# A hybrid decoder layer: output projection by pairs of column blocks, adaLN sums kept in their weight tiles, the second norm of tile 0 among tile 1's last products

## The chip, the cores and the metric

The kernel runs on one core of one Trainium2 chip. The metric is device time in microseconds, from runs of the whole program; the profile is of one further execution. The engines are called TensorE (PE, matrix products), VectorE (DVE), ScalarE (ACT), GpSimd (POOL) and SyncE (SP, which here issues most DMAs).

## What is computed

One layer for 256 tokens of width 2048, all in float32, followed by a final RMSNorm:

```
mod = silu(c) @ w_ada + b_ada          -> shift, scale, gate for the mixer and for the FFN
h   = rms_norm(x) * (1 + scale_m) + shift_m
p   = h @ w_in                         -> column blocks for a GLA group (4 heads) and an HGRN2 group (8 heads)
y   = concat(GLA heads, HGRN2 heads) @ w_out
x   = x + gate_m * y
h   = rms_norm(x) * (1 + scale_f) + shift_f
x   = x + gate_f * (silu(a) * u) @ w_ffn_out,   a, u = split(h @ w_ffn_in)
out = rms_norm(x)
```

Each head's output is normed and multiplied by silu of its gate block before the concatenation.

## The kernel before

**Products.** The 256 tokens are two tiles of 128 (t = 0, 1). A float32 operand is written as a high part, rounded to the fast matrix format, and a low part, the remainder; a product is the sum of three matmuls (`products_of`, L243 to L256: low times high, high times high, high times low). Weights come from memory in half-chunks of 128 x 1024 (`load_ahead`, L216, issued on SyncE's queue, at most 5 ahead), ACT makes the high part (L209) and DVE or POOL the low part (L210). `low_on_pool` (L233) says by the number of the half-chunk which of the two engines takes it: 0 to 111 are the input projection, 112 to 143 the output projection, from 144 on the feed-forward weights. `next_half` (L193) keeps the splits 3 half-chunks ahead of the products, and further ahead for the few named in `EARLY_SPLIT`, whose parts lie in slabs instead of the 4 split buffers.

**Order.** A scheduler orders the instructions of each engine by the order in the program and by its own estimate of when operands and buffers are there; each engine then runs its list in order. `issue_after` places an instruction behind another on the same engine. Buffers of a pool are shared by tag: 33 slabs of 4 KB per partition, 5 raw weight tiles, 4 raw tiles of the adaLN weights, 2 PSUM tiles of two banks (`mm_bank`, `mm_apart`, L258 to L267), 3 single PSUM banks (`bank`) and 1 for the adaLN sums.

**Input projection.** Six groups of rows (`K_GROUPS`), in each of them all column blocks; the gate blocks g0, g1, s0, s1 come last (L722 to L734). Beside the last group and these blocks run three tasks (`gla_group`, `hg_group(0)`, `hg_group(1)`), each advanced once per unit of products. They compute the heads' scores on DVE, ACT and PE, the heads' outputs (`head_outputs`), and in `gated` (L547) the product with the gate block (L549), four transposes per pair of 128 columns on PE (L283) and the split into y (L271, L272). The slabs of y are taken in `gated`.

**adaLN stream.** `ada_sums` (L109) streams 512 columns of w_ada in 8 loads of two row blocks and accumulates row block times c on DVE into one PSUM bank (L127); the last accumulation goes into a slab. `ada_channel` (L134) reduces it over the partitions with matmuls against ones (L147) and makes shift and scale; `ada_gate` (L161) starts from a slab that POOL sets to zero and the bias is loaded into, and reduces with a matmul (L180). `Spread` deals out the steps of this stream evenly over the units of products: 51 steps over 30 units for the second norm's first four column blocks and the mixer's gate.

**Output projection.** All tasks are run to their end in the program (L735) before it. Then four column blocks of 512, one after the other, each over the row groups 8, 12, 0, 4 (`OUT_ORDER`: the HGRN2 halves g0, g1, then the GLA halves s0, s1). After a block, DVE multiplies by the gate and adds x (L754, L755), ACT squares and sums (L757). After block 3, whose last two row groups are one unit and whose tile 1 is done in two halves of 256 columns, come the sums, the power -1/2 on POOL (L295) and the diagonal matrices (L353) for both tiles. The first two row blocks of h for the feed-forward part are then made by matmuls against the diagonal (`normed`, L359), the affine step on ACT and DVE (L420, L418) and the split:

```python
    for t in range(NT):
        c = slice(t * P, (t + 1) * P)
        for j in range(2):
            normed(pts[j][:, :, c], x1[0][:, t], 2 * j, diag_y[t])
            for i in range(2):
                affine(pts[j][:, i, c], 1, 2 * j + i, j == 1)
        for j in range(2):
            h2_made = split_pair(pts[j][:, :, c], h2[j][..., c])
```

**Feed-forward part.** The first six pairs of hidden blocks are computed in four row groups (q = 0 to 3), with the adaLN stream beside them; the first unit takes both blocks of a pair at once (L794 to L797). The rest and the second projection follow, then the final norm.

Of the kernel before, what the change touches and what calls it, by code (L numbers as in the profile page):

```python
# [17 lines left out]
F32 = mybir.dt.float32  # L18
# [4 lines left out]
ALU = mybir.AluOpType  # L23
# [27 lines left out]
MIXER_LOW = (76, 116)  # L51

# [6 lines left out]
def hybrid_layer(ctx: ExitStack, tc: tile.TileContext, x, c, w_ada, b_ada, norm_mix_w, w_in,  # L59
# [49 lines left out]
    def ada_sums(name, out, bias, *parts):  # L109
# [5 lines left out]
        for k0 in range(0, KT, 2):  # L115
# [13 lines left out]
            yield  # L129
# [4 lines left out]
    def ada_channel(which, ka, kb, then=None):  # L134

        n = kb - ka
        sums = slab(f"sums{which}_{ka}", (P, 2, n * P))
        shift, scale = (lambda v, s=s: v[..., 3 * which + s, ka * P:kb * P] for s in range(2))
        if n == 2:
            yield from ada_sums(f"ada{which}_{ka}", sums.rearrange("p s n -> p (s n)"), None, shift, scale)  # L140
        else:
            for s, part in enumerate((shift, scale)):
                yield from ada_sums(f"ada{which}_{ka}_{s}", sums[:, s], None, part)
        pa = pad.tile([P, 2, n], F32, tag="acc", name=f"pada{which}_{ka}")
        for s in range(2):
            for j in range(n):
                nc.tensor.matmul(pa[:, s, j:j + 1], sums[:, s, j * P:(j + 1) * P], ones[:, 0:1],  # L147
                                 start=True, stop=True)
# [11 lines left out]

    def ada_gate(which, half, store):  # L161
# [3 lines left out]
        nc.sync.dma_start(out=gate[0:1], in_=b_ada_v[:, 3 * which + 2, 1024 * half:1024 * (half + 1)]  # L165
                          .rearrange("o (b n) -> o b n", b=2))
        for b in range(2):
            c0 = 1024 * half + 512 * b
            yield from ada_sums(f"adag{which}_{half}_{b}", gate[:, b], gate[:, b],
                                lambda v: v[..., 3 * which + 2, c0:c0 + 512])  # L170
        passes = [(ones, gate)]
        if which:
            hi, lo = (split.tile([P, 2, 512], F32R, tag=n, name=f"{n}_gate{half}") for n in ("hi", "lo"))
            nc.scalar.activation(hi, gate, AF.Copy)
            nc.vector.tensor_tensor(out=lo, in0=gate, in1=hi.bitcast(F32), op=ALU.subtract)
            passes = [(ones_r, lo), (ones_r, hi)]
        for b in range(2):
            pg = pad.tile([P, 512], F32, tag="acc", name=f"pgate{which}_{half}_{b}")
            for i, (one, part) in enumerate(passes):
                nc.tensor.matmul(pg, one, part[:, b], start=i == 0, stop=i == len(passes) - 1)  # L180
# [10 lines left out]
    last_mm = [None]  # L191

    def next_half():  # L193

        i = n_used[0]
        n_used[0] += 1
        while True:
# [537 lines left out]
    while tasks:  # L735
        advance()
# [174 lines left out]
```

## Time and profile before

| | |
|---|---|
| median of 3 runs | 1284.21 us (1283.5 to 1285.42) |
| the profiled execution | 1284.97 us |
| its span, first to last instruction | 1283.1 us |
| TensorE matmuls, busy | 1228.3 us |
| VectorE, busy | 882.7 us |
| ScalarE, busy | 601.5 us |
| GpSimd, busy | 355.1 us |
| mean granted TensorE clock | 0.990 |

The profile is of one execution, and its times are from the start of the span. A wait is put down to the instruction whose signal came last. The granted clock is the share of full speed that TensorE was allowed in a stretch. The busy time of TensorE is modelled from starts and sizes, so starts are the surer thing to read.

### The profile page before, as it was taken

What the parts mean: (1) busy time and instruction counts of PE and PEld (TensorE: products, weight loads), DVE (VectorE), ACT (ScalarE), POOL (GpSimd) and SP (SyncE); (2) the same over time, 40 slices, a digit from 0 to 9 for tenths busy, and PEclk for the clock granted to TensorE, in tenths of its full rate; (3) what the DMA queues carried; (4) which work ended last, traced back from release to release, by engine and by line L of the source; (5) the groups of instructions that cost most, each with busy time, mean ns of one, the idle gap of its engine ahead of it and who ended that gap; (6) DMA issues with size and microseconds to landing.
All of it is one profiled execution on the core that took longest, in us unless ns stands there. A gap on an engine that the chain in (4) does not pass through costs nothing.

```text
span 1283.1 us, 16035 instructions
## 1 busy us (share of the span) xinstructions
PE 1228.3 (96%) x5811; PEld 1025.5 (80%) x5811; DVE 882.7 (69%) x1055; ACT 601.5 (47%) x746; POOL 355.1 (28%) x168
## 2 busy tenths in 40 slices
PE   2999999999997999899999999899999999999996
PEld 2888888888886788688888888788888888888886
DVE  5499986579999873658793799796555454445554
ACT  5644444496643444455343455434334444444443
POOL 4677766500000477365656000000000000000010
PEclk9999999999998999899999999999999999999998
DMA  9999999745577797599897687795666556655662
GB/s 342 350 341 353 355 333 317 253 132 164 178 260 236 262 391 269 190 356 339 309 366 242 214 280 268 253 357 192 197 192 193 185 190 194 187 188 186 196 196 84
DMA packets 178535, 323.65 MB, mean 252 GB/s; under 512 B 12688, under 2 KB 29684, under 8 KB 178456
## 3 DMA queue, kind: packets, MB, share of 16 engines
q1 hardware_dynamic: 175800, 317.33, 73.1%
q10 hardware_dynamic: 2464, 5.24, 1.2%
q8 instruction: 46, 0.75, 0.2%
q14 instruction: 33, 0.27, 0.1%
q0 software_dynamic: 192, 0.06, 0.0%
HBM read 320.49 MB, written 2.10 MB: 251 GB/s over the span
## 4 chain that ended last, share of the span: by engine, by line
PE 60%; DMA 2%; DVE 2%; issue 1%; POOL 1%; ACT 1%; SPq 0%; POOLq 0%; ACTq 0%; DVEq 0%
PE mm_f L256 18%; PE mm_f L254 18%; PE mm_f L255 18%; PE mm_out L254 1%; PE mm_out L255 1%; PE mm_out L256 1%; DMA wada<-in_w_ada_dram 1%; PE pthid L283 1%; DMA raw_f_b<-in_w_ffn_in_dram 1%; PE pth L359 1%; DVE lo_f_a L210 1%; DVE accada L127 0%; POOL lo_out_b L210 0%; PE pada L147 0%; DMA fw<-in_final_norm_w_dram 0%
## 5 line engine op out<-in xcount | busy, mean ns | idle before, releaser
L209 ACT ACTIVATE hi_f_a<-raw_f_a 128x1024 fp32r<-128x1024 f32 x132 | 140.1, 1061 | 337.8 <-PE mm_f L255 319.3
L210 DVE TENSOR_TENSOR lo_f_a<-raw_f_a,hi_f_a 128x1024 fp32r<-128x1024 f32 x116 | 151.8, 1309 | 208.7 <-ACT hi_f_a L209 208.1
L127 DVE SCALAR_TENSOR_TENSOR accada<-wada,c_act,accada 128x512 f32<-128x512 f32 x224 | 168.6, 753 | 18.0 <-DMA wada<-in_w_ada_dram 12.9
L209 ACT ACTIVATE hi_f_b<-raw_f_b 128x1024 fp32r<-128x1024 f32 x132 | 140.0, 1061 | 52.5 <-PE mm_f L255 44.3
L254 PE MATMUL mm_f<-hi_f_a,h 128*128 128x512 f32 x352 | 138.9, 395 | 1.1 <-DVE pf L805 0.6
L256 PE MATMUL mm_f<-lo_f_a,h 128*128 128x512 f32 x352 | 138.2, 393 | 0.0
L255 PE MATMUL mm_f<-hi_f_a,h 128*128 128x512 f32 x352 | 137.8, 391 | 0.0
L256 PE MATMUL mm_f<-lo_f_b,h 128*128 128x512 f32 x352 | 137.6, 391 | 0.0
L254 PE MATMUL mm_f<-hi_f_b,h 128*128 128x512 f32 x352 | 137.1, 390 | 0.0
L255 PE MATMUL mm_f<-hi_f_b,h 128*128 128x512 f32 x352 | 137.1, 389 | 0.0
L854 POOL TENSOR_TENSOR xr<-xr,fw 128x512 f32<-128x512 f32 x6 | 8.8, 1462 | 458.0 <-ACT junkf L851 458.0
L210 DVE TENSOR_TENSOR lo_f_b<-raw_f_b,hi_f_b 128x1024 fp32r<-128x1024 f32 x99 | 122.4, 1237 | 16.9 <-ACT hi_f_b L209 9.6
L210 POOL TENSOR_TENSOR lo_f_b<-raw_f_b,hi_f_b 128x1024 fp32r<-128x1024 f32 x33 | 80.1, 2427 | 44.9 <-ACT hi_f_b L209 44.9
L127 DVE SCALAR_TENSOR_TENSOR accadag<-wadag,c_act,accadag 128x512 f32<-128x512 f32 x112 | 84.2, 751 | 3.4 <-DMA wadag<-in_w_ada_dram 1.8
L254 PEld LDWEIGHTS mm_f<-hi_f_a,h 128*128 128x128 f32 x352 | 66.7, 189 | 15.7 <-ACT hi_f_a L209 1.4
L256 PEld LDWEIGHTS mm_f<-lo_f_a,h 128*128 128x128 f32 x352 | 66.5, 189 | 13.8
L255 PEld LDWEIGHTS mm_f<-hi_f_a,h 128*128 128x128 f32 x352 | 66.5, 189 | 13.6
L255 PEld LDWEIGHTS mm_f<-hi_f_b,h 128*128 128x128 f32 x352 | 66.1, 188 | 13.8
L256 PEld LDWEIGHTS mm_f<-lo_f_b,h 128*128 128x128 f32 x352 | 66.1, 188 | 13.5
L254 PEld LDWEIGHTS mm_f<-hi_f_b,h 128*128 128x128 f32 x352 | 66.1, 188 | 13.3
L254 PE MATMUL mm_f<-hi_f_b,hid 128*128 128x512 f32 (+1 forms) x186 | 70.6, 380 | 3.7 <-ACT hi_f_b L209 3.7
L256 PE MATMUL mm_f<-lo_f_b,hid 128*128 128x512 f32 (+1 forms) x186 | 70.8, 381 | 0.2 <-DVE lo_f_b L210 0.2
(392 smaller groups left out, 2755.3 us busy)
## 6 DMA issues: line engine op xcount, KB each, us to landing
wada<-in_w_ada_dram SPq DMA_DIRECT2D x96, 512.0 KB, 6.0
raw_f_a<-in_w_ffn_in_dram SPq DMA_DIRECT2D x88, 512.0 KB, 4.5
raw_f_b<-in_w_ffn_in_dram SPq DMA_DIRECT2D x88, 512.0 KB, 3.5
wadag<-in_w_ada_dram SPq DMA_DIRECT2D x64, 512.0 KB, 5.6
raw_f_a<-in_w_ffn_out_dram SPq DMA_DIRECT2D x44, 512.0 KB, 4.8
raw_f_b<-in_w_ffn_out_dram SPq DMA_DIRECT2D x44, 512.0 KB, 3.9
wada<-in_w_ada_dram SPq DMA_DIRECT2D x64, 256.0 KB, 6.2
raw_out_a<-in_w_out_dram SPq DMA_DIRECT2D x16, 512.0 KB, 6.4
```

The source lines that it names most:

```text
L127: nc.vector.scalar_tensor_tensor(out=dst, in0=raw[:, j], scalar=ck, in1=acc if k else bias, op0=ALU.mult, op1=ALU.add)
L209: for ins in (nc.scalar.activation(hi, raw, AF.Copy), eng.tensor_tensor(out=lo, in0=raw, in1=hi.bitcast(F32), op=ALU.subtract)):
L210: eng.tensor_tensor(out=lo, in0=raw, in1=hi.bitcast(F32), op=ALU.subtract)):
L254: nc.tensor.matmul(o, xl, hi[:, j, c], start=first and i + j == 0, stop=False)
L255: nc.tensor.matmul(o, xh, hi[:, j, c], start=False, stop=False)
L256: last_mm[0] = nc.tensor.matmul(o, xh, lo[:, j, c], start=False, stop=end)
L283: nc.tensor.transpose(pt[:, j, t * P:(t + 1) * P], src[:, t, (j0 + j) * P:(j0 + j + 1) * P], ident)
L359: nc.tensor.matmul(pt[:, j], src[:, (j0 + j) * P:(j0 + j + 1) * P], diag, start=True, stop=True)
L854: nc.gpsimd.tensor_tensor(out=xt, in0=xt, in1=fw[b // 2][:, b % 2], op=ALU.mult)
```

## The change

The output projection runs in units (column block, row groups): blocks 0 and 1 in turn through all row groups, then block 2, then block 3, and the weights are loaded in that order. The tasks that make y are no longer run to their end first: the second HGRN2 group's transposes and splits wait for unit 0, those of s0 for unit 2 and of s1 for unit 4, behind the last product issued, and only then are y's slabs taken. The adaLN sums stay in the raw weight tile that held their last rows; the mixer's gate takes its slab after its first sum, without a zeroed start, and adds the bias to one row of the sum. The adaLN steps are 16 per channel of four blocks, dealt out in three runs. Half-chunks 134 to 149 have all their low parts on DVE. Block 3's tile 1 has its second half in a single bank; amid that half's products (at its third half-chunk) the program now has the residual of tile 0, its norm rows, and the making of h for tile 0. Tile 1's norm rows follow the last product, and its h is made after the first feed-forward unit's products of tile 0. The split of `f1_0_1_0` and what follows it is held back until then. Cut to what matters:

```diff
+NORM_LOW = (134, 150)
...
-    def ada_sums(name, out, bias, *parts):
+    def ada_sums(name, bias, *parts, out=None):
...
-                dst, ck = out if k == KT - 1 else acc, c_act[:, k:k + 1]
+                dst, ck = acc, c_act[:, k:k + 1]
+                if k == KT - 1:
+                    dst = raw[:, j] if out is None else out
...
-            yield
+            if k0 < KT - 2:
+                yield
+        return dst
...
-        sums = slab(f"sums{which}_{ka}", (P, 2, n * P))
         if n == 2:
-            yield from ada_sums(f"ada{which}_{ka}", sums.rearrange("p s n -> p (s n)"), None, shift, scale)
+            both_sums = yield from ada_sums(f"ada{which}_{ka}", None, shift, scale)
+            sums = [both_sums[:, s * n * P:(s + 1) * n * P] for s in range(2)]
         else:
+            sums = []
             for s, part in enumerate((shift, scale)):
-                yield from ada_sums(f"ada{which}_{ka}_{s}", sums[:, s], None, part)
+                part_sums = yield from ada_sums(f"ada{which}_{ka}_{s}", None, part)
+                sums.append(part_sums)
+                if s == 0:
+                    yield
...
+    def ada_gate_late(which, half, store):
+        gate = None
+        for b in range(2):
+            sums = yield from ada_sums(f"adag{which}_{half}_{b}", None,
+                                       lambda v: gate_part(v, which, half, b))
+            if gate is None:
+                gate = slab(f"adag{which}_{half}")
+                gate_bias(gate, which, half)
+            nc.vector.tensor_tensor(out=sums[0:1], in0=sums[0:1], in1=gate[0:1, b], op=ALU.add)
+            pg = pad.tile([P, 512], F32, tag="acc", name=f"pgate{which}_{half}_{b}")
+            nc.tensor.matmul(pg, ones, sums, start=True, stop=True)
+            nc.scalar.activation(gate[:, b], pg, AF.Copy)
+            store[2 * half + b] = gate[:, b]
+            yield
...
+    def split_ahead(n):
+
         while True:
             load_ahead()
             early = 4 if pending and pending[0][1][:-2] in EARLY_SPLIT else 0
-            if not pending or n_split[0] >= i + 1 + SPLIT_AHEAD + early:
+            if not pending or n_split[0] >= n + early or pending[0][1] == split_held[0]:
...
-        return MIXER_LOW[1] <= i < POOL_END and i % 4 != 0
+        return (MIXER_LOW[1] <= i < NORM_LOW[0] or NORM_LOW[1] <= i < POOL_END) and i % 4 != 0
...
+                        behind_it = ()
+                        if between is not None and between[:3] == (t, r, i):
+                            behind_it = between[3]()
+                            between = None
...
+                            with behind(*behind_it):
+                                nc.tensor.matmul(o, xl, hi[:, j, c], start=first and i + j == 0, stop=False)
...
-        ps = [pmm.tile([P, NT, 512], F32, tag="mm", name=f"{name}_{t}") for t in range(NT)]
-        return [[(slice(0, 512), ps[0][:, 0])],
-                [(slice(256 * i, 256 * i + 256), ps[1][:, i, 0:256]) for i in range(2)]]
+        ps = [pmm.tile([P, NT, 512], F32, tag="mm", name=f"{name}_{t}")[:, 0] for t in range(NT)]
+        return [[(slice(0, 512), ps[0])],
+                [(slice(0, 256), ps[1][:, 0:256]), (slice(256, 512), bank(f"{name}_2")[:, 0:256])]]
...
-    for b in range(4):
-        for k0 in OUT_ORDER:
+    OUT_UNITS = [(b, (k0,)) for k0 in OUT_ORDER for b in (0, 1)]
+    OUT_UNITS += [(2, (k0,)) for k0 in OUT_ORDER]
+    OUT_UNITS += [(3, (k0,)) for k0 in OUT_ORDER[:2]] + [(3, OUT_ORDER[2:])]
+    for b, ks in OUT_UNITS:
+        for k0 in ks:
...
-    def gated(on, g, name):
+    def gated(on, g, name, *after):
 
         nc.vector.tensor_tensor(out=g, in0=g, in1=on.rearrange("p t h d -> p t (h d)"), op=ALU.mult)
-        res = []
-        for j in range(2):
-            y = act_slab(f"y_{name}_{j}")
-            split_pair(transpose_pair(g, 2 * j, f"pty_{name}_{j}"), y)
-            res.append(y)
+        yield from until(*after)
+        res = [act_slab(f"y_{name}_{j}") for j in range(2)]
+        with tc.issue_after(last_mm[0].ins) if after else nullcontext():
+            for j in range(2):
+                split_pair(transpose_pair(g, 2 * j, f"pty_{name}_{j}"), res[j])
         return res
...
-        acts[4 + 2 * i], acts[5 + 2 * i] = gated(on, parts[f"g{i}"], f"g{i}")
+        acts[4 + 2 * i], acts[5 + 2 * i] = yield from gated(on, parts[f"g{i}"], f"g{i}", *("out0",)[:i])
...
-            acts[2 * i], acts[2 * i + 1] = gated(ons[i], parts[f"s{i}"], f"s{i}")
+            acts[2 * i], acts[2 * i + 1] = yield from gated(ons[i], parts[f"s{i}"], f"s{i}",
+                                                            ("out2", "out4")[i])
...
-            side = Spread(chain(ada_channel(1, 0, 4), ada_gate(0, 0, gate_m), ada_gate(0, 1, gate_m)),
-                          51, len(grouped) + n_late + 8)
+            side = Spread(chain(ada_channel(1, 0, 4), ada_gate_late(0, 0, gate_m), ada_gate_late(0, 1, gate_m)),
+                          (16, 6), (16, len(grouped) + n_late - 6), (16, 9))
...
+    def norm_rows(t):
+        diag_y[t] = row_diag(row_rms(ssy[:, t, 0:4 + t], f"y{t}"), f"y{t}")[0]
+
+    def first_h2(t):
...
+        ins = [normed(pts[j][:, :, c], x1[0][:, t], 2 * j, diag_y[t]) for j in range(2)]
...
+    def first_rows():
+
+        with behind(*split_ins["f1_0_0_0_b"]):
+            residual(3, 0, 0)
+        norm_rows(0)
+        return first_h2(0)[1:]
+
+    for u, (b, ks) in enumerate(OUT_UNITS):
+        while not all(k // 2 + i in acts for k in ks for i in range(2)):
+            advance()
+        first, last = b not in psts, ks[-1] == OUT_ORDER[-1]
+        if first:
+            psts[b] = mm_apart(f"mm_out_{b}") if b == 3 else mm_bank(f"mm_out_{b}")[1]
+            x1[b] = slab(f"xr{b}")
+            nc.scalar.dma_start(out=x1[b], in_=xv[:, :, b * 512:(b + 1) * 512])
+        products(psts[b], acts, [k for k0 in ks for k in (k0, k0 + 2)], first, last,
+                 (1, 1, 2, first_rows) if b == 3 and last else None)
+        finished.add(f"out{u}")
+        advance()
+        side.tick()
+        if last and b < 3:
+            for t in range(NT):
+                residual(b, t, 0)
+    side.finish()
+    with behind(made_m[0]):
+        residual(3, 1, 0)
+    with behind(*h2_made[0]):
+        residual(3, 1, 1)
+    norm_rows(1)
+    make_h2 = make_h(1, x1, diag_y, h2)
+    split_held[0] = None
+    with behind(*h2_made[0]):
+        split_ahead(n_used[0] + 4)
+
+    def second_rows():
+        with behind(last_mm[0]):
+            return first_h2(1)
...
-                with tc.issue_after(made_r[0].ins), tc.issue_after(made_d[0].ins), \
-                        tc.issue_after(h2_made.ins):
-                    products_of([(pst, (0, 2)) for _, pst in pss], h2, True, True)
+                products_of([(pst, (0, 2)) for _, pst in pss], h2, True, True, (1, 0, 0, second_rows), False)
```

## Rows read from the trace of the kernel before

**Rows 1.** The page: busy shares, two costly groups, one kind of DMA issue
```profile
PE 1228.3 (96%) x5811; PEld 1025.5 (80%) x5811; DVE 882.7 (69%) x1055; ACT 601.5 (47%) x746; POOL 355.1 (28%) x168
L210 DVE TENSOR_TENSOR lo_f_a<-raw_f_a,hi_f_a 128x1024 fp32r<-128x1024 f32 x116 | 151.8, 1309 | 208.7 <-ACT hi_f_a L209 208.1
L127 DVE SCALAR_TENSOR_TENSOR accada<-wada,c_act,accada 128x512 f32<-128x512 f32 x224 | 168.6, 753 | 18.0 <-DMA wada<-in_w_ada_dram 12.9
wada<-in_w_ada_dram SPq DMA_DIRECT2D x96, 512.0 KB, 6.0
```

**Rows 2.** Waits of TensorE: line <- releaser: us in total, times, longest
```profile
PE pty_g L283 <- DVE p_g L549: 8.1, 1, 8.1
PE pth L359 <- DVE h L272: 3.9, 1, 3.9
PE pty_s L283 <- DVE y_s L272: 0.9, 1, 0.9
PE pth L359 <- ACT diagy L353: 0.9, 1, 0.9
PE mm_out L254 <- DVE y_s L272: 0.8, 1, 0.8
PE pgate L180 <- ACT adag L181: 0.3, 1, 0.3
```

**Rows 3.** Stretches: length, busy us (instructions) of each engine, PEclk, DMA share, GB/s
```profile
404.75:411.57 6.82, 3.80 (x18) 3.83 (x19) 6.75 (x13) 2.11 (x3) 0.00 (x0) 0.50 0.69 228
517.39:524.21 6.82, 4.82 (x13) 4.00 (x14) 1.33 (x4) 3.97 (x8) 2.92 (x2) 0.50 0.00 0
300.00:399.66 99.66, 98.81 (x550) 85.29 (x548) 96.42 (x140) 55.21 (x89) 2.60 (x2) 1.00 0.66 212
399.66:491.50 91.84, 81.74 (x363) 66.71 (x364) 71.47 (x100) 39.95 (x68) 45.54 (x21) 0.96 0.84 295
436.00:491.50 55.50, 55.50 (x246) 45.32 (x246) 39.37 (x48) 24.64 (x31) 33.56 (x14) 1.00 0.89 322
```

**Rows 4.** Timeline of VectorE, last product of the second HGRN2 group's output
```profile
406.40 1.22 DVE L549 TENSOR_TENSOR p_g<-p_g,p_i 128x1024 f32<-128x1024 f32 x1
```

**Rows 5.** Timeline of ScalarE, evacuations of s0 and s1, a square at the norm
```profile
410.23 1.02 ACT L731 ACTIVATE p_s<-mm_in_s 128x1024 f32<-128x1024 f32 x1
433.41 1.02 ACT L731 ACTIVATE p_s<-mm_in_s 128x1024 f32<-128x1024 f32 x1
510.78 0.61 ACT L757 ACTIVATE junky<-xr 128x512 bf16<-128x512 f32 x1
```

**Rows 6.** Timeline of TensorE, end of tile 0 of block 3, first norm products
```profile
507.31 0.39 PE L256 MATMUL mm_out<-lo_out_b,y_s 128*128 128x512 f32 x1
514.34 1.16 PE L359 MATMUL pth<-diagy,xr 128*128 128x128 f32 x8 [0.90 <-ACT diagy L353]
```

**Rows 7.** Timeline of VectorE around the second norm
```profile
507.73 0.70 DVE L754 TENSOR_TENSOR mm_out<-mm_out,adag 128x512 f32<-128x512 f32 x1 [3.51 <-PE mm_out L256]
508.47 0.69 DVE L755 TENSOR_TENSOR xr<-mm_out,xr 128x512 f32<-128x512 f32 x1
511.52 0.16 DVE L301 TENSOR_REDUCE ss_y<-ssy 128x1 f32<-128x4 f32 x1 [2.36 <-ACT junky L757]
522.27 0.42 DVE L272 TENSOR_TENSOR h<-pth,h 128x256 fp32r<-128x256 f32 x1 [2.61 <-ACT h L271]
```

**Rows 8.** Groups of ScalarE, 507 to 523 us: busy us, mean ns, idle before
```profile
L420 ACT ACTIVATE pth<-pth,shiftT,scaleT 128x128 f32<-128x128 f32 x4 | 1.7, 427 | 0.8 <-PE pth L359 0.8
L271 ACT ACTIVATE h<-pth 128x256 fp32r<-128x256 f32 x3 | 1.0, 373 | 0.0
L353 ACT ACTIVATE diagy<-ident,r_y 128x128 f32<-128x128 f32 x2 | 0.8, 402 | 3.4 <-POOL r_y L295 3.4
```

**Rows 9.** Timeline of GpSimd, the power of the first norm rows
```profile
513.30 0.55 POOL L295 TENSOR_TENSOR r_y<-m_y,neg_half 128x1 f32<-128x1 f32 x1
```

**Rows 10.** Waits of SyncE's queue, 530 to 760 us
```profile
SPq L119 <- DVE accada L127: 30.4, 38, 1.7
```

More of the change, by code (lines that the diff above doesn't have):

```diff
@@ L164, in ada_gate @@
         nc.gpsimd.memset(gate, 0.0)
-        nc.sync.dma_start(out=gate[0:1], in_=b_ada_v[:, 3 * which + 2, 1024 * half:1024 * (half + 1)]
-                          .rearrange("o (b n) -> o b n", b=2))
+        gate_bias(gate, which, half)
         for b in range(2):
[L168 to L176, printed above, removed]
+            yield from ada_sums(f"adag{which}_{half}_{b}", gate[:, b],
+                                lambda v: gate_part(v, which, half, b), out=gate[:, b])
+            yield
+        hi, lo = (split.tile([P, 2, 512], F32R, tag=n, name=f"{n}_gate{half}") for n in ("hi", "lo"))
+        nc.scalar.activation(hi, gate, AF.Copy)
+        nc.vector.tensor_tensor(out=lo, in0=gate, in1=hi.bitcast(F32), op=ALU.subtract)
         for b in range(2):
             pg = pad.tile([P, 512], F32, tag="acc", name=f"pgate{which}_{half}_{b}")
-            for i, (one, part) in enumerate(passes):
-                nc.tensor.matmul(pg, one, part[:, b], start=i == 0, stop=i == len(passes) - 1)
+            for i, part in enumerate((lo, hi)):
+                nc.tensor.matmul(pg, ones_r, part[:, b], start=i == 0, stop=i == 1)
             nc.scalar.activation(gate[:, b], pg, AF.Copy)
@@ L191, in hybrid_layer, with behind, next_half @@
     last_mm = [None]
-    def next_half():
+    split_ins = {}
+    split_held = ["f1_0_1_0_a"]
+    @contextmanager
+    def behind(*instructions):
+        with ExitStack() as stack:
+            for ins in instructions:
+                stack.enter_context(tc.issue_after(ins.ins))
+            yield
+    def next_half(ahead=True):
         i = n_used[0]
         n_used[0] += 1
+        if ahead:
+            split_ahead(i + 1 + SPLIT_AHEAD)
+        return ready.pop(i)
+    def split_ahead(n):
         while True:
@@ L591, in hybrid_layer, with __init__ @@
     class Spread:
-        def __init__(self, gen, steps, units):
-            self.gen, self.steps, self.units, self.i, self.done = gen, steps, units, 0, 0
+        def __init__(self, gen, *runs):
+            self.gen, self.i, self.done = gen, 0, 0
+            self.want, total = [], 0
+            for steps, units in runs:
+                self.want += [total + steps * (i + 1) // units for i in range(units)]
+                total += steps
         def tick(self):
+            want = self.want[min(self.i, len(self.want) - 1)]
             self.i += 1
-            want = self.steps * self.i // self.units
             while self.done < want:
```

104 lines of the change are left out of this document (46 added, 58 removed).

## The prediction

> **What bounds the kernel now.** I read the page's busy shares first: TensorE is busy 96% of the span [rows 1], so the change can only pay where TensorE stands still or runs at its lower clock. Next the waits of TensorE, longest first [rows 2]. Leaving out the start-up waits and one in the hidden-layer stage, which the change leaves alone, three places stand out. The transposes of the second HGRN2 group's gated output (pty_g) wait 8.1 us for DVE; around 430 to 435 us there are 0.9 and 0.8 us for the first GLA half (pty_s, mm_out), and 0.3 us at the gate's matmul; at the second norm (pth) 3.9 and 0.9 us. Third, the stretches with the clock [rows 3]. Twice the granted clock is 0.50, that is 1.2 of 2.4 GHz, each time after one of these standstills: 404.75 to 411.57 with 3.80 us of TensorE work in it, and 517.39 to 524.21 with 4.82 us. Work at half clock takes twice as long, so returning to full clock gives 1.9 and 2.4 us. What is to be won is 8.1 + 1.9, then 0.9 + 0.8 + 0.3, then 3.9 + 0.9 + 2.4: 10.0, 2.0 and 7.2 us, together 19.2.
>
> **The first wait, 10.0 us.** TensorE ends the input projection at 399.66 and next in its queue stand the transposes of p_g, whose last DVE product runs from 406.40 to 407.62 [rows 4]. Behind them stand output products that need only the first HGRN2 group. They could not go ahead for a second reason: both PSUM tiles were still held by s0 and s1, evacuated only at 410.23 and 433.41 by ACT [rows 5], although their products were long done. Each evacuation follows just behind the splits of an earlier y (y_g, y_s), so I read them as waiting for slabs in the order in which slabs are asked for. The change asks for the y slabs only when their turn comes, and takes no sums slab. Then s0 and s1 are evacuated as they finish, and the unit of block 0 with rows 8 runs at 399.66. A unit is 24 matmuls; 246 matmuls take 55.5 us in a stretch without a gap [rows 3], so 5.4 us. The transposes now come after that unit, at 405.1, where p_g is still 2.5 us off. If the scheduler puts block 1's unit ahead, nothing is lost; if it puts the transposes there, up to 2.5 us is. The order of before shows it expected p_g by the end of the input projection, 8 us too early, so it will likely put them right there: I take 2.0 (DVE has one accumulation less in between), ends 0 and 2.5.
>
> **The second, 2.0 us.** With units of blocks 0 and 1 alternating, two units (10.8 us) lie between a transposition's release and the unit that reads it: y_s0 is released after unit 2 and read by unit 4, y_s1 after 4, read by 6. Before, only the product just done lay between. These waits go; cost 0, covered by units 3 and 5 as long as DVE delivers, which is the rival below.
>
> **The norm, 7.2 us.** Tile 0 of block 3 ends with the matmul at 507.31, 507.70 [rows 6]. From there the chain is 0.70 and 0.69 on DVE, 0.74 from the start of the square to the start of the sum, 0.16 and about as much again for the scaling, 0.55 on POOL, 0.40 on ACT for the diagonal [rows 5, 7 to 9]: 3.4 us and some 0.3 for eight hand-overs. Before, ACT stood in front of it with a split that waited for its load, and the square began only at 510.78, 1.6 us after its input. The change keeps that split back. TensorE has 24 + 12 products of 256 columns to run meanwhile, at half of 55.5 / 246 = 0.226 us each [rows 3]: 4.1 us against 3.7, so the first transposing products (1.16 us [rows 6]) should find their diagonal. The remaining 12 products, 1.4 us, with the second bank's own part cover most of the affine and split steps; I take 0 there, ends 0 and 0.6. Tile 1's norm rows run beside the first 24 feed-forward products of tile 0 (5.4 us), and suffice. But its transposing products stand behind the last of those, and nothing is queued between them and tile 1's own products. The wait there is new: two affines of 0.43, the ACT split 0.37, the DVE split 0.42 [rows 7, 8], 1.65 us and 0.2 for hand-overs, less the 0.5 us in which TensorE still fills the second bank: 1.3 us, ends 0.8 and 2.0. It is too short to expect the clock to fall. Net of this part: 7.2 - 1.3.
>
> **Small edits.** The bias of each gate block becomes an addition on one row of 512: not shown before; between 0.16 (a tiny sum) and 0.69 (512 columns on all rows) [rows 7], I take the upper end as columns set the length: 4 x 0.69 = 2.8 us on DVE. The memsets of two gate slabs leave POOL, where nobody on the path waited for them: 0. Twelve low parts of splits 134 to 149 move from POOL to DVE, at 1.31 us each [rows 1]; about four of them before block 2 ends, 5.2 us. TensorE's own work is unchanged, and so is SyncE's count of loads; only the order of the w_out loads follows the units. Changed ticks of the adaLN stream in the input projection: one step fewer per channel, 0, hidden by matmuls that are gapless there.
>
> **DVE in the shortened stretch.** From 399.66 to 491.50 DVE is busy 71.47 us of 91.84 [rows 3]. With 2.8 and 5.2 more it has 79.5 in 91.84 - 12.0 + 2.0 = 81.8, or 97%. That is as full as it is from 300 to 399.66 (96.42 of 99.66), where TensorE loses 0.85 us. So it need not cost much: I take 1.5, ends 0 and 4.
>
> **Sums left in the weight tile.** A raw tile of the adaLN stream is now given back when TensorE has read the sum, not when DVE has written it; with four column blocks, the first part's tile stays through eight further loads, so three of four buffers turn. SyncE issues weight loads in one queue with these, and a load that waits holds those behind it. In the first feed-forward stretch SyncE already waits 38 times, 30.4 us in all, at most 1.7, for such a buffer, while TensorE's list shows no wait for it [rows 2, 10]. I take 1.2 us, ends 0 and 4.
>
> **Sum.** 19.2 - 2.0 - 1.3 - 1.5 - 1.2 = 13.2 us. The rows are of an execution of 1284.97 us (span 1283.1 and 1.9 around it); the median of the runs is 1284.21, 0.76 lower. 1284.97 - 13.2 = 1271.8, on the median's footing 1271.0. With every cost at its low end it is 18.4 us, 1265.8; with every cost at its high end (2.5, 2.6, 4, 4) 6.1 us, 1278.1.
>
> **Rivals.** *DVE becomes the bound.* DVE is 97% full ahead of the stretch already. If the y chains arrive as late as they did, relative to DVE's work, TensorE stands in front of unit 4, or of block 3's second PSUM tile, which waits for block 2's residual and so for the last gate. For it: mm_out waited for y_s even behind a standstill of 8 us [rows 2]. Against: DVE still idles 20.4 us in the stretch, and gate sums of the second half now come later. The first two gains are lost, the norm's 5.9 stays: 1284.2 - 5.9 = 1278.3. Chance 0.20. The Trainium skill, Perfetto Trace Analysis, section Identifying the Most-Contended Engine, says that occupancy finds VectorE's bound and that the engine with the highest occupancy is the one to optimize; TensorE's headroom it judges by weight loads. By that rule, with DVE at 97% and weight loads at 86% from 300 to 399.66, this rival would be the forecast; the trace agrees only in part, as TensorE loses 0.85 us there.
>
> *The order isn't what the lines say.* The scheduler may put the norm's products where the diagonal isn't ready, or the transposes early. If tile 0's norm stalls TensorE among tile 1's last products as before (3.9 + 0.9 + 2.4 back), 1271.0 + 5.9 = 1276.9; if the first gap stays instead, about 1279. Chance 0.10.
>
> *Slower: the adaLN stream starves the queue.* Six channels have four column blocks, 48 loads that turn over three buffers. At 0.8 us more for each, the mean of the 38 waits above (30.4 / 38), SyncE's queue is 38 us later in all. The five raw tiles read ahead absorb some; it decides from the point where half of it reaches the splits, 19 us of TensorE's time: 1284.2 - 14.4 + 19 = 1288.8. For it: one queue, in order, for all weights. Against: ten units of 5.4 us have 16 loads, one in 3.4 us, and three buffers that take 6.0 us to land [rows 1] and two sums of 0.753 us each give one in 2.5. Chance 0.13.
>
> **Numbers.** The forecast has 0.57, with its own range 1265.8 to 1276. Faster or slower means by over 0.2% (2.6 us), about what a measurement of this kernel can tell from none. Faster: the forecast, 0.17 of DVE's rival, 0.06 of the order's: 0.80. Same: 0.07, the bad ends of these two. Slower: 0.13. The range takes in DVE's rival and leaves out most of the last: 1265.5 to 1280.
>
> **What would show it.** Right: no wait of pty_g over 2.5 us; evacuations of s0 near 383 and of s1 near 400; granted clock 1.00 from 33 us to past the norm; two transposing products in the last products of block 3; a wait of about 1.3 us before tile 1's feed-forward products. Wrong: DVE full from 400 to 480 and TensorE waiting for y_s or mm_out; SyncE waiting for TensorE at the adaLN loads, with gaps at the group ends; or evacuations still late, which would make the slab reading false.

## The result and the profile after

| | before | after |
|---|---|---|
| median, same chip | 1284.82 us | 1269.91 us (1267.65 to 1270.69, 4 runs) |
| ratio | | 0.988, 95% interval 0.9866 to 0.9893 |
| profiled execution | 1284.97 us | 1267.65 us |
| its span | 1283.1 us | 1265.9 us |

The change makes the kernel 14.9 us faster; 1271.0 had been predicted. The profiled execution is the fastest of its four runs, 2.3 us under their median; so the two traces differ by 17.3 us where the medians differ by 14.9. Of the 17.2 us between their spans, 14.7 lie ahead of the second feed-forward unit and 2.5 behind it.

First the waits of TensorE after the change, from 400 us to the second feed-forward unit, without the 0.5 us at that unit's own start, which both kernels have (line <- releaser: us in total, times, longest):

```profile
PE mm_f L306 <- DVE h L324: 1.4, 1, 1.4
PE mm_f L306 <- ACT hi_f_a L255: 1.1, 1, 1.1
PE pgate L190 <- DVE wadag L188: 0.8, 1, 0.8
PE pth L412 <- ACT diagy L406: 0.7, 1, 0.7
PE mm_f L308 <- DVE lo_f_a L256: 0.5, 1, 0.5
```

Against [rows 2], the 8.1 us for p_g and both waits for y_s are gone. The gate's matmul waits 0.8 instead of 0.3. At the norm the first products wait 0.7 instead of 0.9, a wait of 1.4 stands in place of the 3.9, and two waits are new: 1.1 and 0.5 for the split of `f1_0_1_0`. Both half-clock stretches of [rows 3] are gone.

Three stretches of the trace after, read as [rows 3]; the middle one is the end of the input projection, the last the output projection's first 90 us:

```profile
230.00:300.00 70.00, 67.14 (x370) 55.80 (x369) 57.34 (x82) 51.99 (x77) 13.48 (x6) 1.00 0.74 249
300.00:401.52 101.52, 101.31 (x560) 87.21 (x559) 96.53 (x145) 57.94 (x100) 3.68 (x2) 1.00 0.64 198
401.52:491.50 89.98, 89.17 (x413) 73.23 (x412) 72.47 (x90) 43.47 (x67) 33.88 (x15) 1.00 0.86 293
```

and the first of them in the kernel before:

```profile
230.00:300.00 70.00, 69.00 (x368) 56.61 (x367) 45.89 (x61) 51.26 (x78) 14.32 (x6) 1.00 0.57 185
```

From 230 to 300 us VectorE (third busy number) does 11.5 us more than it did. From 401.52 to 491.50 it is busy 72.47 of 89.98 us, 81%. The prediction had 97% for a stretch of 81.8 us; over the first 81.8 us of this one it is 68.00, 83%. What moved is seen in VectorE's timeline. The second norm's first four column blocks have two sums, one for the shift and one for the scale. Before, their last accumulations (`sums`) and the first one of the mixer's gate (`accadag`) are late:

```profile
288.54 0.74 DVE L127 SCALAR_TENSOR_TENSOR sums<-wada,c_act,accada 128x512 f32<-128x512 f32 x1
373.21 0.74 DVE L127 SCALAR_TENSOR_TENSOR sums<-wada,c_act,accada 128x512 f32<-128x512 f32 x1
382.04 0.76 DVE L127 SCALAR_TENSOR_TENSOR accadag<-wadag,c_act,adag 128x512 f32<-128x512 f32 x1
```

After (the sums now end in the raw tile `wada`; the last line is the product that the first wait was for):

```profile
238.73 0.74 DVE L131 SCALAR_TENSOR_TENSOR wada<-wada,c_act,accada 128x512 f32<-128x512 f32 x1
258.91 0.75 DVE L131 SCALAR_TENSOR_TENSOR wada<-wada,c_act,accada 128x512 f32<-128x512 f32 x1
285.53 0.75 DVE L128 TENSOR_SCALAR accadag<-wadag,c_act 128x512 f32<-128x512 f32 x1
402.47 1.21 DVE L605 TENSOR_TENSOR p_g<-p_g,p_i 128x1024 f32<-128x1024 f32 x1
```

The second sum is done 114 us earlier. Before, the stream stood still for 51 us at the end of the first one (the accumulation ahead of it is at 237.22), and the 16 accumulations of the second came mostly one by one between VectorE's other work. p_g's product ends at 403.68, 2.2 us after the input projection's end at 401.5; before it was 8.0 us after [rows 3, 4]. ScalarE's timeline has the evacuations of s0 and s1, against 410.23 and 433.41 in [rows 5]:

```profile
377.60 1.03 ACT L792 ACTIVATE p_s<-mm_in_s 128x1024 f32<-128x1024 f32 x1
402.46 1.01 ACT L792 ACTIVATE p_s<-mm_in_s 128x1024 f32<-128x1024 f32 x1
```

TensorE's timeline has the transposes of p_g inside the products (no wait in brackets), the gate's matmul, and the norm:

```profile
416.95 0.60 PE L335 MATMUL pty_g<-ident,p_g 128*128 128x128 f32 x4
419.06 1.12 PE L190 MATMUL pgate<-wadag,ones 128*128 128x512 f32 x2 [0.81 <-DVE wadag L188]
420.02 0.60 PE L335 MATMUL pty_g<-ident,p_g 128*128 128x128 f32 x4
...
500.42 1.16 PE L412 MATMUL pth<-diagy,xr 128*128 128x128 f32 x8 [0.66 <-ACT diagy L406]
507.15 0.50 PE L306 MATMUL mm_f<-hi_f_a,h 128*128 128x512 f32 x1 [1.15 <-ACT hi_f_a L255]
508.41 0.50 PE L308 MATMUL mm_f<-lo_f_a,h 128*128 128x512 f32 x1 [0.53 <-DVE lo_f_a L256]
510.80 1.05 PE L412 MATMUL pth<-diagy,xr 128*128 128x128 f32 x8
513.27 0.50 PE L306 MATMUL mm_f<-hi_f_a,h 128*128 128x512 f32 x1 [1.41 <-DVE h L324]
```

The transposing products of tile 0's norm stand among the last products of block 3's tile 1 and wait 0.66 us. The last wait is the 1.3 us that the prediction had for tile 1's h. The 1.15 and 0.53 us were not foreseen.

### The profile page after: what moved, and what is told of

The parts are those of the page before. It is cut to its first block, busy times and chain, and to the rows that moved or that the text cites. A ratio compares the mean times of both kernels' runs of the same rounds, so it can differ in the third digit from the quotient of the medians.

```text
span 1265.9 us, 16022 instructions
## 1 busy us (share of the span) xinstructions
PE 1222.6 (97%) x5811; PEld 1020.5 (81%) x5811; DVE 887.9 (70%) x1071; ACT 603.3 (48%) x747; POOL 324.9 (26%) x154
## 4 chain that ended last, share of the span: by engine, by line
PE 57%; DVE 1%; ACT 1%; issue 1%; DMA 1%; ACTq 0%; POOLq 0%; POOL 0%; DVEq 0%
PE mm_f L306 18%; PE mm_f L308 18%; PE mm_f L307 18%; PE pthid L335 1%; DMA wada<-in_w_ada_dram 1%; PE pth L412 1%; DVE lo_f_a L256 0%; PE pada L157 0%; DVE accada L131 0%; PE pgate L210 0%; ACT hi_f_a L255 0%; ACT hi_f_b L255 0%; DVE pf L893 0%; ACT hi_gate L205 0%; ACT pf L891 0%
## 5 line engine op out<-in xcount | busy, mean ns | idle before, releaser
L256 DVE TENSOR_TENSOR lo_f_a<-raw_f_a,hi_f_a 128x1024 fp32r<-128x1024 f32 x117 | 145.7, 1245 | 211.8 <-ACT hi_f_a L255 211.2
L256 DVE TENSOR_TENSOR lo_f_b<-raw_f_b,hi_f_b 128x1024 fp32r<-128x1024 f32 x102 | 126.1, 1236 | 16.4 <-ACT hi_f_b L255 9.1
L256 POOL TENSOR_TENSOR lo_f_b<-raw_f_b,hi_f_b 128x1024 fp32r<-128x1024 f32 x30 | 72.7, 2423 | 38.0 <-ACT hi_f_b L255 38.0
L306 PE MATMUL mm_f<-hi_f_b,hid 128*128 128x512 f32 (+1 forms) x186 | 70.9, 381 | 3.7 <-ACT hi_f_b L255 3.7
L307 PE MATMUL mm_f<-hi_f_b,hid 128*128 128x512 f32 (+1 forms) x186 | 70.7, 380 | 0.0
```

The lines of the kernel that those rows point to most:

```text
L256: eng.tensor_tensor(out=lo, in0=raw, in1=hi.bitcast(F32), op=ALU.subtract))
L306: nc.tensor.matmul(o, xl, hi[:, j, c], start=first and i + j == 0, stop=False)
L307: nc.tensor.matmul(o, xh, hi[:, j, c], start=False, stop=False)
```

## The experiments

Twelve kernels ran, each timed against the kernel before on the same chip. The changed kernel ran again among them:

> The changed kernel itself, on the same chip as the three others, to compare them with: 1269.9 us, within 1.2.

Measured 1268.21 us (1267.37 to 1270.96), ratio 0.9876 (0.9853 to 0.9899). Two medians of one kernel thus differ by 1.7 us, and below about 2 us I go by the traces, which have their own scatter from the clock (last section). For the stages after the input projection I compare the time from its end to the start of the second feed-forward unit, "the stretch": 118.0 us in both traces of the changed kernel.

**Were the evacuations late for slabs?**

```diff
+        res = [act_slab(f"y_{name}_{j}") for j in range(2)]
         yield from until(*after)
-        res = [act_slab(f"y_{name}_{j}") for j in range(2)]
```

> The changed kernel, but y's slabs are asked for before the wait for their unit, as the kernel before did. Slab theory (the late evacuations of s0 and s1 in the kernel before came from slabs handed out in the order asked): p_s is evacuated some 8 us or more later than 377.6 and 402.5 us, the output projection's first products start later than 401.5 us, and the wait of about 8 us comes back with up to 1.9 us of half clock: 1278 to 1280 us. Rival (the sums' slabs alone, which the change no longer takes, gave room enough; the order of asking is nothing): evacuations where they are, 1270 us, within 1.2.

Measured 1268.81 us, ratio 0.9878 (0.9857 to 0.9898): no change. p_s was evacuated at 379.4 and 404.3. So the order in which slabs are asked for does not by itself make s0 and s1 late.

**Transposes of p_g right behind the input projection.**

```diff
-  yield from gated(on, parts[f"g{i}"], f"g{i}", *("out0",)[:i])
+  yield from gated(on, parts[f"g{i}"], f"g{i}")
```

> The changed kernel, but the transposes of p_g are not held behind unit 0: as before they stand right behind the input projection, and in ACT's list the evacuations of s0 and s1 stand behind the splits of y_g, as they did in the kernel before (asking for y's slabs early, run above, moved neither). Queue theory (the evacuations were late before because ACT's list had them behind splits that waited for p_g's DVE product): TensorE waits some 2 us for p_g (its product ended 2.2 us after the input projection in the changed kernel), then again for s0's evacuation, which now comes after 405 us instead of at 377.6: 4 to 7 us in all and perhaps a half-clock stretch, 1274 to 1278 us. Rival (slabs made them late, and slabs are free now): s0 is evacuated near 378 all the same, only the 2 us wait comes: 1272 us.

Measured 1274.09 us, ratio 0.9915 (0.9899 to 0.9932), some 4 to 6 us lost. In TensorE's waits and ScalarE's group (duration min/median/max, first and last start):

```profile
PE pty_g L335 <- DVE p_g L605: 2.5, 1, 2.5
```

```profile
L792 ACT ACTIVATE p_s<-mm_in_s x2: 1030/1036/1042, 403.4 to 404.3; 128x1024 f32<-128x1024 f32 x2
```

In ScalarE's timeline the split of y_g stands just ahead of s0's evacuation, here and in the kernel before:

```profile
402.46 1.08 ACT L323 ACTIVATE y_g<-pty_g 128x512 fp32r<-128x512 f32 x2 [2.31 <-PE pty_g L335]
```

```profile
408.89 0.60 ACT L271 ACTIVATE y_g<-pty_g 128x512 fp32r<-128x512 f32 x1 [7.57 <-PE pty_g L283]
```

s0 is late again, at 403.4. The slabs of y are asked for at the same place as in the run above, where s0 was evacuated at 379.4; only the transposes differ, and with them the place of y_g's splits in ScalarE's list. That place is what makes s0 late here, and the kernel before has the same order. It cost no wait of its own; the 2.5 us, a half-clock stretch from 402.96 to 406.38 and later waits (1.1 at a product, 1.6 at the norm) make the loss.

**Blocks 0 and 1 one by one.**

```diff
-  OUT_UNITS = [(b, (k0,)) for k0 in OUT_ORDER for b in (0, 1)]
+  OUT_UNITS = [(b, (k0,)) for b in (0, 1) for k0 in OUT_ORDER]
...
-  ("out2", "out4")[i])
+  ("out1", "out2")[i])
```

> The changed kernel, but blocks 0 and 1 one after the other as before (the transposes of p_g, s0, s1 behind units 0, 1, 2). Theory (one unit of 5.4 us doesn't cover transposes and splits of y and DVE's product, two do): TensorE waits for y_g, y_s0 and y_s1 at units 1, 2 and 3, some 1 to 2.5 us each and more for y_g, as p_g's DVE product ends later than one unit after the first: 1274 to 1279 us, with a half-clock stretch if one wait passes some 5 us. Rival (only the late evacuations held the kernel before): no new wait over 1 us, 1269 to 1271 us.

Measured 1274.99 us, ratio 0.9926 (0.9911 to 0.9941): 5 to 7 us lost, the stretch 125.5 us. Its waits:

```profile
PE pgate L190 <- DVE wadag L188: 3.9, 1, 3.9
PE mm_out L306 <- DVE y_s L324: 1.2, 1, 1.2
```

with a half-clock stretch from 415.54 to 422.37. The time is the theory's, but the largest wait is not one for y: it is the gate's matmul, among the transposes, waiting for VectorE. Of the waits for y only the 1.2 us came. The half clock came with a wait of 3.9 us, not only with one of over 5.

**Sums in slabs again.** First all channel sums, then only the two of the channel that is made beside the last group of the input projection:

```diff
+  kept = slab(f"sums{which}_{ka}", (P, 2, n * P))      # second run: only for which, ka == 1, 0
...
-  part_sums = yield from ada_sums(f"ada{which}_{ka}_{s}", None, part)
+  part_sums = yield from ada_sums(f"ada{which}_{ka}_{s}", None, part, out=kept[:, s])
```

> The changed kernel, but the channel sums of adaLN are written to a slab again, as before. Cost term of the prediction (1.2 us, ends 0 and 4, for raw tiles held longer): SyncE's waits for adaLN buffers become fewer and the time falls by 1.2, 1268.7 us. Slab theory (the slab that the sums no longer take is what lets s0, s1 and y through): evacuations later than 378 and 403 us and waits of y_g or mm_out, 1272 to 1280 us. Null (neither): 1270 us within 1.2, evacuations where they are.

> The changed kernel, but only the sum of the second norm's first four column blocks (the one that is made beside the last group of the input projection) is written to a slab again. Stream theory (this sum has to wait for a slab, and the adaLN stream behind it with it, so that some 12 us of DVE work, the gate's first accumulations, move from before 300 us to after 380, in front of p_g's product): the gate's first accumulation starts near 380 us instead of 285.5, p_g's product ends 8 us or more after the input projection instead of 2.2, TensorE waits some 5 us for y_g with a half-clock stretch: 1275 to 1279 us. Rival (the loss with all sums in slabs came from the earlier channels, the 2.3 us wait at 173 us and its half clock): 1270 us, no wait of y_g.

Measured 1279.33 us, ratio 0.9948 (0.993 to 0.9967), and 1274.31, ratio 0.9926 (0.991 to 0.9942). The cost term falls outright: the edit that I had charged 1.2 us is worth 9 to 11, and 4 to 6 of it lies with the two sums of that one channel. The second run, VectorE's timeline and TensorE's waits:

```profile
277.15 0.74 DVE L131 SCALAR_TENSOR_TENSOR sums<-wada,c_act,accada 128x512 f32<-128x512 f32 x1
366.56 0.75 DVE L131 SCALAR_TENSOR_TENSOR sums<-wada,c_act,accada 128x512 f32<-128x512 f32 x1
376.30 0.75 DVE L128 TENSOR_SCALAR accadag<-wadag,c_act 128x512 f32<-128x512 f32 x1
```

```profile
PE pty_g L337 <- DVE y_g L326: 5.0, 1, 5.0
```

Only the place of these two sums was changed. The first moved from 238.73 to 277.15, 37 us behind the accumulation ahead of it; the second moved from 258.91 to 366.56, and the gate's accumulations behind it, as they stood before the change. p_g's product ended at 408.9 (7.5 us after the input projection), and VectorE's split of y_g came 5.0 us late, followed by a half-clock stretch from 425.74 to 429.15. With all sums in slabs the same 5.0 us stands there, and a wait of 2.3 us for a block of the first norm's h at 173.5 us, with its half-clock stretch (175.48 to 178.89), comes on top. s0 and s1 were evacuated at 384.1 and 406.0 there, so slabs taken by sums did not make them late either. That the sum waited for a slab to come free is read from the edit; no row names the buffer.

**Is VectorE the bound of the output projection?**

```diff
-NORM_LOW = (134, 150)
+NORM_LOW = (116, 150)
```

> The changed kernel, but DVE also takes the low parts of splits 116 to 133, 13 of them that POOL had, at 1.25 us each: 16 us more DVE work from about 395 to 460 us, where DVE stands idle some 6 us from 401.5 to 446 and 12 from 446 to 491. DVE theory (DVE is close to being the bound of this stretch, the prediction's first rival): most of what doesn't fit, 6 to 10 us, comes to TensorE as waits for lo_out, y or pgate: 1276 to 1280 us. Rival (two units between a transposition and its use cover it): within 2 us of the changed kernel.

Measured 1271.16 us, ratio 0.9899 (0.9884 to 0.9914): 1 to 3 us lost. The output projection in two stretches:

```profile
401.00:446.00 45.00, 43.88 (x204) 35.87 (x203) 41.90 (x56) 21.83 (x37) 2.01 (x2) 1.00 0.86 289
446.00:492.00 46.00, 46.00 (x216) 37.91 (x215) 39.84 (x48) 21.20 (x30) 0.00 (x0) 1.00 0.88 296
```

The 16 us of work made VectorE only some 9 us busier there, 81.7 of 91.0 us instead of 72.5 of 90.0, because several of its other instructions took less time with GpSimd idle (last section). So this is a test at 90%, not at 97%. TensorE's new waits are 1.1 us for y_g, and 2.0 instead of 0.7 at the norm; the 0.8 at the gate's matmul went. The prediction's first rival did not come true, and at 90% VectorE is not yet the bound.

**One raw tile fewer for the adaLN stream.**

```diff
-N_ADA = 4
+N_ADA = 3
```

> The changed kernel with three raw tiles for the adaLN stream instead of four, so two where a first sum is held. Starving theory (the prediction's slower rival: SyncE's one queue stands at the adaLN loads and holds the weight loads behind them): TensorE waits for splits whose loads come late, in the feed-forward part above all, 5 to 15 us: 1275 to 1285 us. Slack theory (three had slack to spare, the queue runs far enough ahead): SyncE waits longer at these loads, but TensorE not more than 1.5 us: 1269 to 1271.5 us.

Measured 1284.41 us (ten runs, 1283.15 to 1291.7), ratio 1.0007 (0.9995 to 1.0018): the whole gain is gone. The profiled execution is the one of 1291.7, so 7.3 us of what it shows are not in the median. SyncE's waits from 530 to 760 us, in the changed kernel and then here:

```profile
SPq L121 <- DVE accada L131: 23.4, 29, 2.7
...
SPq L121 <- PE pada L157: 10.7, 6, 3.4
```

```profile
SPq L121 <- DVE accada L131: 39.6, 35, 3.1
SPq L121 <- PE pada L157: 11.9, 6, 3.5
SPq L121 <- DMA wada<-in_w_ada_dram: 8.0, 9, 2.3
```

and TensorE's three longest waits here from 400 to 860 us:

```profile
PE mm_f L306 <- ACT hi_f_b L255: 8.7, 4, 5.8
PE pgate L190 <- DVE wadag L188: 3.4, 2, 2.9
PE pada L157 <- DVE wada L131: 2.7, 1, 2.7
```

One buffer fewer costs the whole gain, but not in the way that the rival had. VectorE's waits for the stream's own loads, in the changed kernel and here, and a wait of ScalarE here:

```profile
DVE accada L131 <- DMA wada<-in_w_ada_dram: 26.5, 23, 3.4
```

```profile
DVE accada L131 <- DMA wada<-in_w_ada_dram: 71.5, 48, 5.2
ACT pth L475 <- DVE scaleT L165: 13.4, 5, 5.4
```

The sums come late, and TensorE waits for them (`pada`, `pgate`), ScalarE for the scale made from them (0.9 us in the changed kernel). ScalarE's longest wait for a feed-forward weight is 1.3 us here and 1.4 in the changed kernel, so in the feed-forward part no weights are seen to be held up. The 5.8 us within the 8.7 is the changed kernel's wait of 3.7, for a split that stands behind the gate's. A further 6.3 us were lost before the output projection, which starts at 407.8 instead of 401.5.

In the changed kernel SyncE does wait six times for TensorE to read a held sum, 10.7 us, as the rival had it, but its waits for VectorE's sums fell from 30.4 us [rows 10] to 23.4, and TensorE waits for none of it.

**The norm's part.** First undone: both tiles' norm stands behind all products, and the split is not held back.

```diff
-    split_held = ["f1_0_1_0_a"]
+    split_held = [None]
...
-  (1, 1, 2, first_rows) if b == 3 and last else None)
+  None)
...
+    residual(3, 0, 0)
     residual(3, 1, 0)
     residual(3, 1, 1)
+    norm_rows(0)
     norm_rows(1)
+    first_h2(0)
+    first_h2(1)
```

> The changed kernel, but the second norm of both tiles after all products of the output projection and ahead of the feed-forward part, as before, and the split of f1_0_1_0 not held. By the two traces (waits and clock at the norm: 5.3 us and 2.4 us of half clock before, 4.2 us and none after) the norm's part is worth 3.5 us: 1273.4 us, with pth waits of 4 to 5 us and the clock at 0.50 after them. By the prediction's own term (7.2 - 1.3) it is worth 5.9: 1275.8. Rival (the norm's part gained nothing that the first wait's end did not bring): 1270 us.

Measured 1271.75 us, ratio 0.9897 (0.9882 to 0.9911), 1.8 to 3.5 us lost; the stretch is 119.6 us, 1.6 longer. The timeline of TensorE:

```profile
504.26 2.07 PE L412 MATMUL pth<-diagy,xr 128*128 128x128 f32 x8 [2.36 <-ACT diagy L406]
507.63 1.22 PE L412 MATMUL pth<-diagy,xr 128*128 128x128 f32 x4 [1.29 <-DVE h L324]
```

Waits of 3.7 us and half clock from 504.23 to 511.06 stand against four waits of 3.8 us and full clock in the changed kernel. So the part saves no standing time; it splits it into pieces after which the clock stayed up in these two traces. It need not: the trace with slabs asked for early has the changed kernel's waits at the norm, half clock behind them, and a stretch of 119.6 us too. The 1.6 us are therefore no more than what the clock alone makes between executions of one norm.

Then without holding back the split:

```diff
-    split_held = ["f1_0_1_0_a"]
+    split_held = [None]
```

> The changed kernel, but the split of f1_0_1_0 is not held back: it stands on ACT ahead of tile 0's square. Theory A (holding it is worth it: its load lands late and the square behind it waits): square and diagonal of tile 0 are 1.5 to 3 us late, the norm's products wait for them, 1271 to 1273 us. Theory B (the load is there in time in the changed kernel; holding it only moves 1.7 us of wait to the first feed-forward unit, 1.15 and 0.53 us): those two waits go and the square is late by at most its 2.1 us on ACT, some of it hidden: 1268.5 to 1270 us.

Measured 1270.73 us, ratio 0.9879 (0.986 to 0.9898), not to be told from the changed kernel. In the trace the 1.15 and 0.53 go, the norm's wait grows from 0.7 to 2.8, and the clock is at half from 505.38 to 508.79; the stretch is 119.2 us, 1.2 longer. That is within the same scatter, so no gain of holding back is shown, and neither theory is wholly right.

**Better: tile 1's h between the two blocks.** The new last number in the brackets names the block ahead of whose first product of tile 0 the h is made.

```diff
-  products_of([(pst, (0, 2)) for _, pst in pss], h2, True, True, (1, 0, 0, second_rows), False)
+  products_of([(pst, (0, 2)) for _, pst in pss], h2, True, True, (0, 0, 0, second_rows, 1), False)
...
```

> The changed kernel, but tile 1's h is made between the two blocks' products of tile 0 in the first feed-forward unit, and not behind both. Theory (the 1.4 us wait there is the chain affine and split with nothing queued beside it; and TensorE stands 1.2 and 0.5 us for the split of f1_0_1_0 just where the transposing products would now be): the 1.4 goes, most of the 1.7 is covered by 1.1 us of transposing products, 2 to 2.7 us less in the trace: 1267.5 us. Rival (tile 1's diagonal isn't there yet, or its affines now stand ahead of the split's second half on ACT and the wait moves there): within 1 us of the changed kernel, 1269 to 1270.5.

Measured 1266.82 us, ratio 0.986 (0.9841 to 0.9878); the stretch is 115.5 us, 2.5 shorter. What is left at the norm:

```profile
PE pth L412 <- ACT diagy L406: 0.9, 2, 0.7
PE mm_f L308 <- DVE lo_f_a L256: 0.5, 1, 0.5
```

The 1.41 and 1.15 us are gone: the transposing products fill the place where TensorE waited for the first half of the split. The 0.53 us for its low part stays, and 0.2 us for tile 1's diagonal is new. To this I added a gate for the feed-forward part made as the mixer's is:

```diff
-  side = Spread(chain(ada_gate(1, 0, gate_f), ada_gate(1, 1, gate_f)), (34, 2 * FFN_GROUPED + 2 * HIDDEN_SPLIT))
+  side = Spread(chain(ada_gate_late(1, 0, gate_f), ada_gate_late(1, 1, gate_f)), (32, 2 * FFN_GROUPED + 2 * HIDDEN_SPLIT))
```

> Tile 1's h between the two blocks' products (as run above, 1266.8 us), and the feed-forward gate made like the mixer's, without the split through the shared split buffers. Theory (the 3.7 us wait near 792 us, which both kernels have, is ACT's list: the split of the next weights stands behind the split of the gate's sum, which waits for DVE): wait and the 3.4 us half-clock stretch after it go, 3.7 + 1.7 less, four float32 gate products of about 0.85 us instead of eight of 0.21 add 1.7: 1263 us. Rival (the split waits for a free split buffer anyway and the wait stays): 1266.8 to 1268.5 us.

Measured 1262.97 us (1261.38 to 1264.07), ratio 0.9834 (0.9819 to 0.9849), some 21 us under the kernel before and 5 to 7 under the changed one. TensorE's list has no wait from 760 to 830 us, where both kernels had one of 3.7 (it ends at 812.99 before and at 797.67 after the change), and the clock stays at full speed there.

## Why the prediction was right, and where it was not

The time was right, 1271.0 for 1269.9, by steps of which some were not; that their errors nearly cancel is luck. In the traces the first wait gave 10.0 us, the second 1.2 and the norm 3.5; waits in the input projection took 1.3 back. The second feed-forward unit starts at 519.48 instead of 534.20, 14.7 us earlier, so 1.3 us are left. They lie in the start-up: the input projection's second block starts at 36.85 us instead of 38.23. No experiment tells whether the change did this; in nine other runs with the same start-up it begins between 36.6 and 38.2. What it had named to look for came: no wait of p_g's transposes, s0 and s1 evacuated at 377.6 and 402.5 (383 and 400 predicted), full clock from 33 us to past the norm.

*The first wait.* The gain of 10.0 us came in full (8.1 us of wait and the half clock). The mechanism was read only half. "I read them as waiting for slabs in the order in which slabs are asked for" is false: asking early moved nothing, and ScalarE's list with the transposes put back made s0 late again. And p_g was 8 us late itself, because VectorE had the gate's sums in front of it; I took that lateness as given. No run undid order and sums together, so how the 10.0 us divide between them is not shown. The cost of 2.0 for transposes that come too early is 0: they went into later products, at 416.95, where p_g had been ready for 13 us.

*Sums left in the weight tile.* This step failed most. "I take 1.2 us, ends 0 and 4" counted only what the held tiles cost. Undone, the edit's net worth is 9 to 11 us: with sums in slabs the stream stood still for 37 to 51 us at one sum, and its later accumulations fell into the stretch where VectorE is full. It is the reason for part of the first wait's end, which I credited to order alone. Blocks in turn (5 to 7 us), the held transposes (4 to 6) and the free stream overlap; they don't add up.

*VectorE's fullness.* 97% was predicted and 83% measured over the same length, since 11.5 us of VectorE's work had moved ahead of 300 us. The cost was 0.8 us, at the gate's matmul, for 1.5. The Trainium skill, Perfetto Trace Analysis, section Identifying the Most-Contended Engine, says that the engine with the highest occupancy is the one to optimize, by which this rival would have been the forecast. The runs do not bear that out here: with VectorE at 90% instead of 81%, 1 to 3 us reached the time.

*Small edits.* The four bias additions took 6.3 us (0.68, 2.84, 2.09 and 0.68), not 2.8; the last section has the reason.

*The second, 2.0 us.* The waits for y_s are gone; with the 0.8 this is a gain of 1.2.

*The norm, 5.9 us net.* Comparing the two traces, waits went from 5.3 to 4.2 us and 2.4 us of half clock went: 3.5. Undone, it is 1.6 in the trace, which the clock alone can make. The 1.3 for tile 1's h was right (1.41). The failed step is "should find their diagonal. The remaining 12 products ... cover most". The products waited 0.66 us for the diagonal, and nothing was charged for the split that is held back, which stands behind tile 1's diagonal on ScalarE (at 506.06) and lets TensorE wait 1.15 and 0.53 us.

*The slower rival.* Its danger, too few raw tiles, was one tile away. Its mechanism was not seen: with three tiles the stream's own loads and sums came late, and no weights of the feed-forward part behind them.

*A gain that was not counted.* `mm_apart`, which now puts tile 1's second half into a bank of its own, also serves the last block of the second projection. VectorE's first multiplication for that tile, before and after:

```profile
1272.89 0.43 DVE L847 TENSOR_TENSOR mm_f<-mm_f,adag 128x256 f32<-128x256 f32 x1 [1.33 <-PE mm_f L256]
```

```profile
1254.15 0.43 DVE L935 TENSOR_TENSOR mm_f<-mm_f,adag 128x256 f32<-128x256 f32 x1 [0.20 <-PE mm_f L308]
```

Before, it follows TensorE's last product, which ends at 1272.86; after, it comes 2.8 us ahead of that product's end at 1256.98. From there to the end of the span it is 10.2 us before and 8.9 us in all thirteen traces with the change: 1.3 us, which the prediction did not count. No run undid this edit alone.

## What to carry to other kernels

When a stream of side work shares a pool with the main work, look at when its steps ran, not only at how much they cost: one output that waits for a buffer can push a whole chain into the stretch where its engine is full. Read an engine's list before blaming a buffer, by looking for what stands just ahead of the late instruction. Where an engine waits for a short chain, move ready work into the place, or move the chain to where the engine waits already.

## What the runs showed of the hardware

The bias addition on one row of 512 takes 0.68 us alone and 2.84 or 2.09 us while GpSimd makes a low part. VectorE, then GpSimd, in the changed kernel:

```profile
381.54 0.68 DVE L188 TENSOR_TENSOR wadag<-wadag,adag 1x512 f32<-1x512 f32 x1 [2.35 <-DMA adag<-in_b_ada_dram]
...
416.16 2.84 DVE L188 TENSOR_TENSOR wadag<-wadag,adag 1x512 f32<-1x512 f32 x1
```

```profile
415.70 2.75 POOL L256 TENSOR_TENSOR lo_out_a<-raw_out_a,hi_out_a 128x1024 fp32r<-128x1024 f32 x1 [1.68 <-ACT hi_out_a L255]
```

With all low parts of the output projection on VectorE the four additions took 0.67 to 0.68 us each, and the 0.8 us wait behind the second one was gone. The Trainium skill, SBUF — State Buffer, section SBUF: two separate sides, says that VectorE with two SBUF inputs and GpSimd take a shared port pair in turn, each for a whole instruction; the trace agrees, as 416.16 + 2.84 lies 0.55 us, about one addition, behind GpSimd's end at 418.45. The third addition, 2.09 us from 444.79, ends 0.54 us behind GpSimd's at 446.34.

The clock is not tied to the length of a wait alone. A wait of 2.0 us at the norm (low parts on VectorE) left it at full speed; 2.8 us (split not held) was followed by 3.4 us at half. With early slabs, where the waits at the norm are those of the changed kernel, one execution had this stretch behind them (columns as in [rows 3]), and the changed kernel's traces had none there:

```profile
510.28:513.69 3.41, 3.41 (x8) 2.74 (x9) 1.04 (x1) 0.00 (x0) 0.00 (x0) 0.50 0.67 180
```

The same execution, and that of the last run, had another 3.4 us at half clock after a wait of 1.12 us near 281 us; the changed kernel waits 1.09 us there and stays at full clock. So some of the 1 to 2 us by which runs of one kernel differ is the clock, and a wait of one length does not cost the same in each execution.
